# Seven block products in place of eight for gate and up of three FFNs and the convolution's input projection

## The chip, the cores and the metric

One NeuronCore of one Trainium2 chip runs the whole program in one launch. The metric is the time of one execution on the device in microseconds. The engines are TensorE (matrix products, "PE", its weight loads "PEld"), VectorE ("DVE"), ScalarE ("ACT"), GpSimd ("POOL") and SyncE ("SP", which issues most of the DMAs).

## The reference

Two layers of a causal decoder trunk, in float32. Each layer is FFN, mixer, FFN; the mixer of layer 0 is a diagonal state space model (S5) with a GLU, that of layer 1 a short gated convolution. 512 prompt tokens and 8 x 8 sample tokens go through the same weights.

```python
def _ffn_half(x, g, w_gu, w_down):
    h = _rmsnorm(x, g)
    gate, up = jnp.split(h @ w_gu, 2, axis=-1)      # w_gu: 1024 x 8192
    return (jax.nn.silu(gate) * up) @ w_down        # w_down: 4096 x 1024

def _conv_mixer(h, buf, w_in, conv_w, w_out):
    gb, gc, v = jnp.split(h @ w_in, 3, axis=-1)     # w_in: 1024 x 3072
    z = gc * v
    ...                                             # three taps along the tokens
    return (gb * conv) @ w_out, ...

# layer i: x += 0.5 ffn(x); x += mixer(rmsnorm(x)); x += 0.5 ffn(x); at the end an rmsnorm
```

## The kernel before, in words

**Layout.** All 576 tokens stay on the chip, features in partitions: `x` is 8 tiles of 128 features x 576 tokens. A product of a 128x128 weight tile with a tile of tokens is done in two halves of 288 columns (`NH`), and each half three times, because a float32 operand is split into a high part rounded to `F32R` and a low remainder: high weight x high tokens, low weight x high tokens, high weight x low tokens (`Step.mm`, line 128).

**Steps.** The work is a list of steps. A step has 8 weight tiles of 128x128, so 8 x 3 x 2 = 48 matmuls. A gate or up step makes one tile of 128 features from the 8 input tiles; a down step takes 4 tiles of h and adds to two tiles of x. One FFN is 8 groups of 8 gate and up steps and 4 down steps; the GLU has 16 steps, the convolution 24 for its input projection (c, v, b) and 8 for its output.

**Weights.** A `Unit` is 1 MB of weights, loaded by one DMA of SyncE into one of two `raw` buffers; it serves two steps. `split` (lines 116 and 117) makes a step's high half `wh` on ScalarE and its low half `wl` on VectorE, in one of four buffers each; it is called three steps ahead (`split_upto(n + 3)`).

**Order.** `tc.manual_schedule()` is on: each engine's instructions run in the order in which the Python code issues them. In the main loop step n is: split of step n+3, matmuls of step n, `finish(n)` with the epilogue. Results go to PSUM tiles of two banks (`[P, 2, 512]`, one bank a half), four of which rotate. The gate epilogue is a product with rstd (L205), Silu (L206) and again rstd (L207); up is a product (L214), the high half of h (L216) and its low half (L217); down adds to x (L223).

**Norms.** `next_norm` scales each final x tile by the norm's g into a high and low `xg` tile (L175, L176) and adds up squares (L168, L169) while the last down steps run; `start` issues the first matmuls of the next stage, then rstd (L182 to L193), which only the epilogues need.

**Buffers.** The pool `actp` has 20 tiles of 128x2x576; xg, h, the mixer's tables and its y take turns in it. The S5 constants lie in a pool that lives to the end, and the convolution borrows one of them (`trig`) for its shifted rows.

Of the kernel before, what the change touches and what calls it, by code (L numbers as in the profile page):

```python
# [33 lines left out]
def trunk_kernel(ctx: ExitStack, tc: tile.TileContext, a, o):  # L34
# [6 lines left out]
    actp = ctx.enter_context(tc.tile_pool(name="actp", bufs=20))  # L41
# [5 lines left out]
    dram = ctx.enter_context(tc.tile_pool(name="dram", bufs=1, space=bass.MemoryType.DRAM))  # L47
    ctx.enter_context(tc.manual_schedule())
# [7 lines left out]
    def ctile(shape, dt, name):  # L56
        return const.tile(shape, dt, name=name, tag=name)

# [15 lines left out]
    # ---------------------------------------------------------------- constants, parameters, x  # L74
# [15 lines left out]
    # ---------------------------------------------------------------- the stream of weights  # L90
# [12 lines left out]
    class Step:  # L103
# [15 lines left out]
        def mm(self, m, k, x, halves=(0, 1)):  # L119
            """The products of weight tile (k, m) with x, into the step's PSUM tile m."""  # L120
# [31 lines left out]
    # ---------------------------------------------------------------- norms  # L152
# [20 lines left out]
    def scaled_in(i, g):  # L173
        t = act(name="xg")
        S.activation(t[:, 0], x[:, i], AF.Copy, scale=g)  # L175
        late.append(lambda: stt(t[:, 1], x[:, i], g, raw32(t[:, 0]), op0=MUL, op1=SUB))  # L176
        return t
# [79 lines left out]
    def next_norm(n):  # L257
        def go(i):
            flush()
            if i == 0:  # L260
                state["xg_next"] = []
            state["xg_next"].append(scaled_in(i, gcol(n, i)))
            square_in(i)
            if i == NT - 1:
                state["xg"] = state["xg_next"]
        return go
# [4 lines left out]
    trig = ctile([P, 2, PAIRS * NK], F32, "trig")  # L271
    cosT, sinT = (trig[:, q].rearrange("p (t k) -> p t k", k=NK) for q in range(2))
    mag8 = ctile([P, PAIRS], F32, "mag8")
    s0 = ctile([P, G, NS], F32, "s0")
    ns = ctile([P, 2, NS, PAIRS], F32, "ns")
    hfin = ctile([P, G], F32, "hfin")
    scr = ctile([P, 2368], F32, "scr")
# [14 lines left out]
    dmask = ctile([P, 16], F32, "dmask")  # L292
    warm = ctile([P, 1], F32, "warm")
    strip = ctile([P, P + TC], F32, "strip")
    exi = ctile([P, PAIRS], I32, "exi")
# [19 lines left out]
    def exp_exact(out, z, t1, t2):  # L315
        """exp by range reduction and a polynomial, to float32's accuracy."""
# [138 lines left out]
    def bg_unit_powers():  # L455
        """cos and sin of 8 theta, their table over chunks, and |a|^8."""
# [56 lines left out]
    def bg_pw_rev():  # L513
        """Powers a^(7-j), j = 0..7, over (j, t) in rows."""
# [62 lines left out]
    def bg_q(i):  # L577
        """Rows of C a^n: real part, and minus the imaginary part."""
# [101 lines left out]
    # ---------------------------------------------------------------- S5: the mixer  # L680
# [8 lines left out]
    def ssm_bounce(i):  # L689
        """g x, from rows (g c) to rows (c j) by way of DRAM; the mean square of each token."""  # L690
# [4 lines left out]
        U = ss["U", i] = act([P, N], F32, "U")  # L695
# [6 lines left out]
    def chunk_rstd():  # L702
        """rstd of token (j, k) in rows (c j), column k."""
# [87 lines left out]
    def ssm_back(i):  # L791
        y = ss["y", i] = act(name="y")
        GP.dma_start(raw32(y[:, 1]), y_d[i].rearrange("g (c j) k -> (g c) (j k)", j=TC))
# [11 lines left out]
    def ssm(n):  # L805
        """The mixer, and the first four steps of the GLU, whose products follow y as it comes."""
# [46 lines left out]
        products((2, 3), (6, 7))  # L853
        state["xg"] = [ss["y", i] for i in range(NT)]
# [24 lines left out]
    # ---------------------------------------------------------------- GLU  # L879
    def glu():  # L880
# [8 lines left out]
        def gate(i):  # L889
            def go(ps):  # L890
# [4 lines left out]
                next_norm(2)(i)  # L895
# [13 lines left out]
    # ---------------------------------------------------------------- short convolution  # L909
    def conv():  # L910
        w_in, w_out = a["conv_w_in"][0], a["conv_w_out"][0]
        g, ps_t = {}, {}
        zp = trig[:, 0, 0:2 * W + N]
        cache = trig[:, 1, 0:128].rearrange("p (i e) -> p i e", e=16)
        zlast = trig[:, 1, 128:272].rearrange("p (i e) -> p i e", e=18)

        def load_cache():
            GP.memset(zp, 0.0)
            state["cache"] = act([16, D], F32, "cache_in")
            GP.dma_start(state["cache"], a["cache_conv"][0].rearrange("s w d -> (s w) d"))  # L920

        def turn_cache():
            t = state.pop("cache")
            ps = psum()
            for i in range(NT):
                T.transpose(ps[:, 0, i * 16:(i + 1) * 16], t[:, i * P:(i + 1) * P], ident[:16, :16])
            S.activation(cache, ps[:, 0, 0:P].rearrange("p (i e) -> p i e", e=16), AF.Copy)

        def scaled(key):
            def go(ps):  # L930
                t = tmpt(name="cv")
                V.tensor_mul(h2(t), ps[:, :, :NH], h2(state["rstd"]))
                g[key] = t
            return go

        def value(i):
            def go(ps):
                scaled(("v", i))(ps)
                z = zp[:, 2 * W:]
                V.tensor_mul(z, g.pop(("c", i)), g.pop(("v", i)))  # L940
                head = zp[:, 0:2 * W].rearrange("p (w k) -> p w k", w=2)
                S.activation(head[:, :, 0:NS], cache[:, i].rearrange("p (s w) -> p w s", w=2), AF.Copy)
                tail = zp[:, 8 * W:].rearrange("p (w k) -> p w k", w=2)
                S.activation(head[:, :, NS + 1:], tail[:, :, NS:W - 1], AF.Copy)
                zl = zlast[:, i].rearrange("p (w e) -> p w e", w=2)
                S.activation(zl[:, :, 0:NS], tail[:, :, 0:NS], AF.Copy)
                S.activation(zl[:, :, NS:], tail[:, :, W - 1:], AF.Copy)
                c = tmpt(name="conv")
                wv = [vecs[:, (GW + k) * 8 + i:(GW + k) * 8 + i + 1] for k in range(3)]
                V.tensor_scalar(c, zp[:, 0:N], wv[0], None, op0=MUL)  # L950
                stt(c, zp[:, W:W + N], wv[1], c, op0=MUL, op1=ADD)
# [362 lines left out]
```

## Time and profile before

| | |
|---|---|
| median of 3 runs | 2908.58 us (2908.33 to 2910.24) |
| span of the profiled execution | 2910.0 us |
| TensorE matmuls | 21694, busy 2872.7 us |
| VectorE, ScalarE busy | 1452.2 us, 799.7 us |
| from DRAM | 260.19 MB, 97 GB/s over the span |

The span runs from the first to the last instruction of one execution. Matmuls overlap in the array, so the mean time of one (296 ns) is longer than the distance between two. Idle time of an engine is put down to what ended it. Rows below are whole lines of the profile; "..." marks lines left out between them.

### The profile page before, as it was taken

How to read it: one execution, taken by the hardware profiler on the slowest of the kernel's cores; microseconds unless marked ns; L12 is line 12 of the kernel's file. 1: busy time of each engine (PE TensorE's matmuls, PEld its weight loads, DVE VectorE, ACT ScalarE, POOL GpSimd, SP SyncE). 2: the span in 40 equal slices, each digit the busy share in tenths (PEclk: the TensorE clock that was granted, in tenths of full speed). 3: DMA queues.
4: the chain of work that ended last, by engine and by line, in shares of the span. 5: the costliest groups of instructions: out<-in, count | busy, mean ns of one | idle time of the engine just before them, and what ended most of it. 6: DMA issues, size and time to landing. Idle time of an engine off the chain costs nothing.

```text
span 2910.0 us, 48733 instructions
## 1 busy us (share of the span) xinstructions
PE 2872.7 (99%) x21694; PEld 2858.2 (98%) x21694; DVE 1452.2 (50%) x1903; ACT 799.7 (27%) x1054; POOL 132.2 (5%) x208
## 2 busy tenths in 40 slices
PE   8999999998999999999999999999999999999998
PEld 8999999998999999999999999999999999999998
DVE  5667655549344444444544444444655544444444
ACT  4222243332332222222332222222323322222223
POOL 3000122102100000000000000000000000000000
PEclk9999999998999999999999999999999999999999
DMA  6355444447223222222222222222123222222221
GB/s 128 95 153 160 128 145 146 125 160 232 76 77 98 75 84 75 88 87 87 73 87 87 74 87 87 76 85 88 59 93 96 74 76 84 87 88 87 78 82 48
DMA packets 227105, 285.15 MB, mean 98 GB/s; under 512 B 17332, under 2 KB 179488, under 8 KB 226864
## 3 DMA queue, kind: packets, MB, share of 16 engines
q1 hardware_dynamic: 217504, 256.86, 28.6%
q0 software_dynamic: 9216, 24.98, 2.9%
q8 instruction: 171, 2.80, 0.4%
q10 hardware_dynamic: 176, 0.20, 0.1%
q14 instruction: 38, 0.31, 0.0%
HBM read 260.19 MB, written 21.80 MB: 97 GB/s over the span
## 4 chain that ended last, share of the span: by engine, by line
PE 96%; DVE 2%; issue 1%; DMA 0%; SPq 0%; ACT 0%; POOLq 0%; ACTq 0%; DVEq 0%
PE ps L128 94%; PE ps L1039 1%; DMA xin<-in_x_prompt_dram 0%; PE ps L785 0%; DVE scr L772 0%; PE ps L611 0%; DVE g L764 0%; DVE scr L773 0%; PE ps L784 0%; DVE xg L1239 0%; PE ps L1062 0%; DVE U L727 0%; PE ps L182 0%; DVE v L766 0%; DVE v L755 0%
## 5 line engine op out<-in xcount | busy, mean ns | idle before, releaser
L128 PE MATMUL ps<-xg,wh 128*128 128x288 f32 x8960 | 1569.2, 296 | 3.0 <-DVE xg L1239 3.0
L128 PEld LDWEIGHTS ps<-xg,wh 128*128 128x128 f32 x8960 | 1323.6, 189 | 6.2 <-DVE xg L1239 3.4
L128 PE MATMUL ps<-xg,wl 128*128 128x288 f32 x4480 | 959.8, 296 | 0.0
L128 PEld LDWEIGHTS ps<-xg,wl 128*128 128x128 f32 x4480 | 722.7, 189 | 0.0
L128 PE MATMUL ps<-h,wh 128*128 128x288 f32 x3968 | 695.2, 296 | 0.0
L117 DVE TENSOR_TENSOR wl<-raw,wh 128x1024 fp32r<-128x1024 f32 x432 | 529.9, 1227 | 232.1 <-ACT wh L116 232.1
L116 ACT ACTIVATE wh<-raw 128x1024 fp32r<-128x1024 f32 x432 | 453.4, 1050 | 613.3 <-PE ps L128 454.1
L128 PEld LDWEIGHTS ps<-h,wh 128*128 128x128 f32 x3968 | 586.2, 189 | 1.3 <-DVE x L223 1.3
L128 PE MATMUL ps<-h,wl 128*128 128x288 f32 x1984 | 424.8, 296 | 0.0
L223 DVE SCALAR_TENSOR_TENSOR x<-ps,x 128x576 f32<-128x576 f32 x248 | 187.1, 757 | 303.0 <-PE ps L128 301.7
L128 PEld LDWEIGHTS ps<-h,wl 128*128 128x128 f32 x1984 | 319.8, 189 | 0.0
L206 ACT ACTIVATE gate<-gate 128x576 f32<-128x576 f32 x128 | 87.7, 686 | 586.4 <-DVE gate L205 578.5
L205 DVE TENSOR_TENSOR gate<-ps,rstd 128x576 f32<-128x576 f32 x128 | 96.9, 757 | 300.9 <-PE ps L128 300.7
L216 ACT ACTIVATE h<-up 128x576 fp32r<-128x576 f32 x128 | 87.7, 685 | 571.8 <-DVE up L214 555.4
L214 DVE TENSOR_TENSOR up<-ps,gate 128x576 f32<-128x576 f32 x128 | 96.8, 757 | 264.3 <-PE ps L128 264.1
L217 DVE TENSOR_TENSOR h<-up,h 128x576 fp32r<-128x576 f32 x128 | 97.1, 758 | 96.9 <-ACT h L216 96.1
L207 DVE TENSOR_TENSOR gate<-gate,rstd 128x576 f32<-128x576 f32 x128 | 97.1, 759 | 96.4 <-ACT gate L206 96.4
L128 PE MATMUL ps<-y,wh 128*128 128x288 f32 x512 | 92.6, 302 | 0.0
L128 PEld LDWEIGHTS ps<-y,wh 128*128 128x128 f32 x512 | 77.8, 194 | 0.0
L128 PE MATMUL ps<-y,wl 128*128 128x288 f32 x256 | 55.8, 300 | 0.0
L920 POOL DMA_DIRECT2D cache_in<-in_cache_conv_dram x1 | 0.5, 525 | 1066.4 <-PE ps L128 1066.4
L128 PE MATMUL ps<-cg,wh 128*128 128x288 f32 x256 | 44.9, 296 | 0.0
(316 smaller groups left out, 1172.7 us busy)
## 6 DMA issues: line engine op xcount, KB each, us to landing
raw<-in_ffn_w_gate_up_dram SPq DMA_DIRECT2D x126, 1024.0 KB, 5.7
raw<-in_ffn_w_down_dram SPq DMA_DIRECT2D x64, 1024.0 KB, 5.1
raw<-in_conv_w_in_dram SPq DMA_DIRECT2D x12, 1024.0 KB, 5.1
raw<-in_ssm_w_glu_dram SPq DMA_DIRECT2D x8, 1024.0 KB, 5.4
pri<-pw_d SPq DMA_DIRECT2D x16, 256.0 KB, 8.8
bri<-bb_d SPq DMA_DIRECT2D x16, 256.0 KB, 8.7
ws_d<-ws POOLq DMA_DIRECT2D x8, 512.0 KB, 4.1
wy_d<-wy POOLq DMA_DIRECT2D x8, 512.0 KB, 2.9
```

What stands on the lines that cost most here:

```text
L116: S.activation(self.wh, src, AF.Copy)
L117: V.tensor_sub(self.wl, src, raw32(self.wh))
L128: T.matmul(self.ps[m][:, b, :NH], wt[:, k, c], x[:, part, b * NH:(b + 1) * NH], start=k == 0 and wt is self.wh and part == 0, stop=k == se ...
L205: V.tensor_mul(h2(t), ps[:, :, :NH], h2(state["rstd"]))
L206: S.activation(t, t, AF.Silu)
L207: V.tensor_mul(t, t, state["rstd"])
L214: V.tensor_mul(h2(t), ps[:, :, :NH], h2(gates.pop(d)))
L216: S.activation(h[:, 0], t, AF.Copy)
L217: V.tensor_sub(h[:, 1], t, raw32(h[:, 0]))
L223: V.scalar_tensor_tensor(h2(x[:, i]), ps[:, :, :NH], 0.5, h2(x[:, i]), op0=MUL, op1=ADD)
L920: GP.dma_start(state["cache"], a["cache_conv"][0].rearrange("s w d -> (s w) d"))
L1039: T.matmul(pst[i][:, 0, :NH], wt[:, k, m * P:(m + 1) * P], hs[k][:, part, cols], start=k == 0 and wt is st.wh and part == 0, stop=k == 3 a ...
```

## The change

The second, third and fourth FFN and the convolution no longer run as steps, apart from down and output products. Their gate, up and input weights are taken in units of 256 columns, and a unit's 1024x256 block is cut in four: 512x128 each (rows of the 8 input tiles alternate between the two halves). The tokens are cut in their two halves of 288. The eight block products of such a 2x2 by 2x2 product are replaced by seven (Strassen's scheme in Winograd's form), on sums of weight blocks and of token blocks; each is 4 x 3 = 12 matmuls of 288 columns, and the results are put together from running sums.

- `Seven` holds a unit. `make_r1`, `make_s12`, `make_r2`, `make_s4` are its weight chunks: sums on VectorE, high half on ScalarE, low half on VectorE. `pump` issues the next chunk as soon as one of four buffers (and one of one for s4) has been given up by the products issued so far.
- `product` issues the 12 matmuls. Q1, S2, S1 and S4 add up in one bank (`x`), S3 and Q4 in a second (`z`); Q2 has its own (`y`). `evacuate` follows each: ScalarE copies bank x after Q1, S2, S1 and S4, VectorE forms the other combinations, and Q4's is followed by the epilogue of the 256 columns (`gate`, `up`, or the convolution's).
- `stage` sets the order: Q1 of a unit, S4 of the one before, S3, Q4 of the one before, S2, Q2, S1; the four down steps of a group come behind S1 of every fourth unit.
- `feed` and `combine` take the place of `next_norm`: each pair of final x tiles is scaled, four sums are made, and seven blocks are split in high and low.
- Pools: S5's constants and `actp` (12 tiles now) are closed when the mixer ends and the new buffers lie in their place; xg, U and y of the earlier stages have a pool of their own, `xgp`.

The core of the diff, new code only:

```diff
+    def pump():
+        while chunks and live[chunks[0].tag] < cap[chunks[0].tag]:
+            c = chunks.pop(0)
+            live[c.tag] += 1
+            c.make()
...
+    class Seven:
+        TERMS = {"Q1": ("r1", 0, 0, "x"), "S3": ("r1", 1, 5, "z"), "S2": ("s12", 0, 4, "x"),
+                 "S1": ("s12", 1, 3, "x"), "Q2": ("r2", 0, 1, "y"), "Q4": ("r2", 1, 6, "z"),
+                 "S4": ("s4", 0, 2, "x")}
...
+        def make_r1(self):
...
+            V.tensor_add(st[:, :, 1], a21, a22)
+            V.tensor_add(a21, a21, a11)
+            V.tensor_add(st[:, :, 0], st[:, :, 1], a11)
+            self.w["r1"] = split_of(v[:, :, 0], 2, wp, ("wh", "wl"))
+
+        def make_s12(self):
+            self.s4f = late_tile("s4f", "s4f", [P, 4, 1, P], F32, "s4f")
+            V.tensor_add(self.s4f[:, :, 0], self.st[:, :, 0], self.v[:, :, 1, 0])
+            self.w["s12"] = split_of(self.st, 2, wp, ("wh", "wl"))
...
+            for k in ks:
+                t = state["tk"][k]
+                for wt, part in ((wh, 0), (wl, 0), (wh, 1)):
+                    T.matmul(ps, wt[:, k, sel], t[:, part, slot],
+                             start=term in ("Q1", "Q2", "S3") and k == 0 and wt is wh and part == 0,
...
+        def evacuate(self, term):
...
+                S.activation(self.q[:, 0], x_, AF.Copy)
+            elif term == "S2":
+                S.activation(self.q[:, 1], x_, AF.Copy)
+            elif term == "Q2":
+                V.tensor_add(self.c[:, 0, 0], self.q[:, 0], self.y)
+            elif term == "S1":
+                S.activation(self.q[:, 2], x_, AF.Copy)
+                stt(self.c[:, 1, 1], self.q[:, 2], -1.0, z_, op0=MUL, op1=SUB)
+            elif term == "S4":
+                S.activation(self.c[:, 0, 1], x_, AF.Copy)
+            elif term == "Q4":
+                stt(self.c[:, 1, 0], self.q[:, 1], -1.0, z_, op0=MUL, op1=SUB)
+                self.after(self.c.rearrange("p a b n -> p a (b n)"))
...
+    def combine(j, ba):
+
+        bt = big([P, 4, NH], "bt")
+        V.tensor_sub(bt[:, 0:3:2], ba[:, 0:3:2], ba[:, 3:4].to_broadcast([P, 2, NH]))
+        stt(bt[:, 1], bt[:, 0], -1.0, ba[:, 2], op0=MUL, op1=SUB)
+        stt(bt[:, 3], bt[:, 1], -1.0, ba[:, 1], op0=MUL, op1=SUB)
+        t = late_tile("tkr" if j < 3 else "tkl", "tk", [P, 2, 7, NH], F32R, "tk")
+        S.activation(t[:, 0, 0:3], ba[:, 0:3], AF.Copy)
+        V.tensor_sub(t[:, 1, 0:3], ba[:, 0:3], raw32(t[:, 0, 0:3]))
+        S.activation(t[:, 0, 3:7], bt, AF.Copy)
+        V.tensor_sub(t[:, 1, 3:7], bt, raw32(t[:, 0, 3:7]))
...
+            items.append(s.item("Q1"))
+            if prev:
+                items.append(prev.item("S4"))
+            items.append(s.item("S3"))
+            if prev:
+                items.append(prev.item("Q4"))
+            items += [s.item("S2"), s.item("Q2"), s.item("S1")]
+            items += inserts.get(n, [])
...
+        def gate(b):
+            def go(c):
+                V.tensor_mul(c, c, spread(state["rstd"]))
+                S.activation(c, c, AF.Silu)
...
+        def up(b):
+            def go(c):
+                g = gates.pop(b)
+                V.tensor_mul(g, g, spread(state["rstd"]))
+                V.tensor_mul(c, c, g)
+                h = late_tile("hp", "hp", [P, 2, 2, N], F32R, "h")
+                S.activation(h[:, 0], c, AF.Copy)
+                V.tensor_sub(h[:, 1], c, raw32(h[:, 0]))
...
+            it.run()
+            for c in it.chunks:
+                c.left -= 1
+                if c.left == 0:
+                    live[c.tag] -= 1
+            pump()
```

In the convolution `value` rescales 256 rows, then does the product, the shifts and the three taps for each of its two tiles; `gateb` multiplies into a float32 tile, which is split in high and low just ahead of the output products.

## Rows read from the trace of the kernel before

**Rows 1.** The page, part 1: busy us, share of the span, instructions.

```profile
PE 2872.7 (99%) x21694; PEld 2858.2 (98%) x21694; DVE 1452.2 (50%) x1903; ACT 799.7 (27%) x1054; POOL 132.2 (5%) x208
```

**Rows 2.** The page's chain that ended last, shares of the span by engine.

```profile
PE 96%; DVE 2%; issue 1%; DMA 0%; SPq 0%; ACT 0%; POOLq 0%; ACTq 0%; DVEq 0%
```

**Rows 3.** Pieces of that chain in order of time: start, length, instruction.

```profile
850.92 614.39 PE ps L128 x4608
```

**Rows 4.** Waits of ScalarE: who waited for whom; total us, times, longest.

```profile
ACT gate L206 <- DVE gate L205: 578.5, 126, 6.5
```

**Rows 5.** Groups by line and shape: busy us, mean ns of one, idle before.

```profile
L117 DVE TENSOR_TENSOR wl<-raw,wh 128x1024 fp32r<-128x1024 f32 x432 | 529.9, 1227 | 232.1 <-ACT wh L116 232.1
L116 ACT ACTIVATE wh<-raw 128x1024 fp32r<-128x1024 f32 x432 | 453.4, 1050 | 613.3 <-PE ps L128 454.1 <-issue 128.1 <-DMA raw<-in_ffn_w_gate_up_dram 25.1
...
L214 DVE TENSOR_TENSOR up<-ps,gate 128x576 f32<-128x576 f32 x128 | 96.8, 757 | 264.3 <-PE ps L128 264.1
...
L206 ACT ACTIVATE gate<-gate 128x576 f32<-128x576 f32 x128 | 87.7, 686 | 586.4 <-DVE gate L205 578.5 <-issue 7.9
...
L175 ACT ACTIVATE xg<-x,vecs 128x576 fp32r<-128x576 f32 x32 | 25.0, 781 | 70.8 <-DVE x L969 32.5 <-DVE x L223 23.9 <-DVE x L894 14.3
...
L1043 DVE SCALAR_TENSOR_TENSOR x<-ps,x 128x288 f32<-128x288 f32 x16 | 7.2, 458 | 9.6 <-PE ps L1039 9.6
...
L951 DVE SCALAR_TENSOR_TENSOR conv<-trig,vecs,conv 128x576 f32<-128x576 f32 x8 | 6.6, 820 | 0.3
...
L413 DVE TENSOR_TENSOR wst<-pri,bri 128x512 f32<-128x512 f32 x8 | 5.5, 693 | 0.3
...
L1051 ACT ACTIVATE sq<-x 128x288 f32<-128x288 f32 x12 | 5.1, 428 | 0.0
```

**Rows 6.** Timeline where one step ends and the next begins: start, length.

```profile
1013.95 0.43 PE L128 MATMUL ps<-xg,wh 128*128 128x288 f32 x2
...
1014.15 1.06 ACT L116 ACTIVATE wh<-raw 128x1024 fp32r<-128x1024 f32 x1 [5.28 <-PE ps L128]
```

**Rows 7.** Timeline of one gate's epilogue and the next weight split.

```profile
1021.34 0.69 ACT L206 ACTIVATE gate<-gate 128x576 f32<-128x576 f32 x1 [6.13 <-DVE gate L205]
...
1021.93 1.04 ACT L116 ACTIVATE wh<-raw 128x1024 fp32r<-128x1024 f32 x1
...
1023.01 1.23 DVE L117 TENSOR_TENSOR wl<-raw,wh 128x1024 fp32r<-128x1024 f32 x1 [0.19 <-ACT wh L116]
```

**Rows 8.** Timeline of two VectorE instructions with nothing to wait for.

```profile
1436.93 0.75 DVE L223 SCALAR_TENSOR_TENSOR x<-ps,x 128x576 f32<-128x576 f32 x1
...
1437.60 0.81 DVE L176 SCALAR_TENSOR_TENSOR xg<-x,vecs,xg 128x576 fp32r<-128x576 f32 x1
```

**Rows 9.** Timeline of the convolution's shifts.

```profile
2092.50 0.31 ACT L944 ACTIVATE trig<-trig 128x126 f32<-128x126 f32 x1 [5.12 <-DVE trig L940]
```

**Rows 10.** Timeline of VectorE over one rstd, its first and last instruction.

```profile
1466.33 0.76 DVE L184 TENSOR_SCALAR var<-ps 128x576 f32<-128x576 f32 x1 [2.60 <-PE ps L182]
...
1473.25 0.76 DVE L193 TENSOR_TENSOR rstd<-r,newt 128x576 f32<-128x576 f32 x1
```

**Rows 11.** Timeline of TensorE, start of the kernel: idle in brackets.

```profile
33.73 0.78 PE L128 MATMUL ps<-xg,wh 128*128 128x288 f32 x4 [1.97 <-DVE xg L1239]
```

**Rows 12.** Timeline of TensorE in the mixer, two gaps.

```profile
668.35 2.19 PE L736 MATMUL ps<-U,ws 128*64 128x72 f32 x32 [3.98 <-issue]
...
688.40 0.62 PE L785 MATMUL ps<-scr,wy 128*128 128x72 f32 x2 [2.63 <-issue]
```

**Rows 13.** Windows of TensorE: stretch, length, busy, granted clock, DMA share, GB/s.

```profile
33.00:35.00 2.00, 1.27 (x9) 1.00 0.83 229
668.00:670.00 2.00, 1.65 (x28) 0.50 1.00 310
690.00:692.00 2.00, 2.00 (x11) 0.50 1.02 410
736.00:738.00 2.00, 2.00 (x11) 0.50 0.43 106
```

More of the change, by code (lines that the diff above doesn't have):

```diff
@@ L47, in trunk_kernel @@
     dram = ctx.enter_context(tc.tile_pool(name="dram", bufs=1, space=bass.MemoryType.DRAM))
+    early, mid_left, late_r = ExitStack(), ExitStack(), ExitStack()
+    xgp = mid_left.enter_context(tc.tile_pool(name="xgp", bufs=8))
+    s5p = early.enter_context(tc.tile_pool(name="s5p", bufs=1, side="right"))
+    actp = early.enter_context(tc.tile_pool(name="actp", bufs=12, side="right"))
     ctx.enter_context(tc.manual_schedule())
@@ new lines, in open_left, with __init__ @@
+    def open_left():
+        mid_left.close()
+        for n, bufs in (("tkl", 1), ("hp", 2), ("s4", 1)):
+            B[n] = late_r.enter_context(tc.tile_pool(name=n, bufs=bufs, side="left", reuse_waits="tile"))
+        cap["s4"] = 1
+    class Chunk:
+        def __init__(self, tag, unit, make):
+            self.tag, self.unit, self.make, self.left, self.made = tag, unit, make, 0, False
+    class Item:
+        def __init__(self, chunks, run):
+            self.chunks, self.run = chunks, run
+            for c in chunks:
+                c.left += 1
@@ L997, in conv @@
-        starts.append(first)
-        steps[first - 12].post = load_cache
-        steps[first - 8].post = turn_cache
-        hs = lambda: [g["h", k] for k in range(NT)]
-        mid = len(steps)
-        for i in range(0, NT, 2):
-            uo = unit(w_out[:, i * P:(i + 2) * P], 8, 2 * P)
-            for s in range(2):
-                steps.append(Step(uo, s, hs, [out(i + s)]))
-        pairs.append(mid)
-        steps[mid + 1].post = rows_out
-    def tail(n):
-        last = steps[n:n + 4]
-        split_upto(n + 3)
+                    T.transpose(ps[:18, 0, k * P:(k + 1) * P], B["c_zlast"][:, hf * 4 + k], ident)
@@ new lines, in conv_items, with first @@
+        items = stage(sevens)
+        st = []
+        for i in range(0, NT, 2):
+            uo = Unit(w_out[:, i * P:(i + 2) * P], 8, 2 * P)
+            st += [Step(uo, s, lambda: [g["h", k] for k in range(NT)], [out(i + s)]) for s in range(2)]
+        cs = [step_chunk(t) for t in st]
+        def first():
+            for k in range(NT):
+                split_cg(k)
+                for t in st[:2]:
+                    t.mm(0, k, g["h", k])
+            for t in st[:2]:
+                t.evac[0](t.ps[0])
+            rows_out()
@@ new lines, in conv_items, with later, tail @@
+        return items + [Item(cs[:2], first)] + [step_item(t, c) for t, c in zip(st[2:], cs[2:])]
+    def later():
+        for it in late_items:
+            while not all(c.made for c in it.chunks):
+                n = len(chunks)
+                pump()
+                assert len(chunks) < n
+            pump()
+            it.run()
[3 more added lines that the diff above has]
+                    live[c.tag] -= 1
+            pump()
+    def tail(last):
@@ L1125, in trunk_kernel @@
     glu()
-    ffn(0, 1, next_norm(3))
-    ffn(1, 0, next_norm(4))
-    conv()
-    ffn(1, 1, lambda i: None)
     steps[last_ffn1 - 5].post = ssm_prefetch
+    late_items = late_ffn(0, 1, feed(3))
+    late_items += late_ffn(1, 0, feed(4), {8: load_cache, 10: turn_cache})
+    late_items += conv_items(feed(5)) + late_ffn(1, 1, None)
+    for it in late_items:
+        for c in it.chunks:
+            if c not in chunks:
+                chunks.append(c)
+                if c.unit not in units:
+                    units.append(c.unit)
     loaded, done = [0], [0]
@@ L1259, in trunk_kernel @@
     n = 0
-    while n < len(steps) - 4:
+    while n < len(steps):
         if n == 0:
@@ L1282, in trunk_kernel @@
         assert not bg or n < last_ffn1 - 5, len(bg)
-    tail(n)
+        if "big" in B and done[0] == len(steps):
+            live["w"] = len(steps) - n + sum(1 for c in made if c.tag == "w")
+            pump()
+    later()
+    late_r.close()
 _INS = ["x_prompt", "x_sample", "state_ssm_re", "state_ssm_im", "cache_conv", "norm_g", "final_norm_g",
```

370 lines of the change are left out of this document (267 added, 103 removed).

## The prediction

> **What bounds the kernel now.** I read the page first. Part 1 shows TensorE busy 99% of the span, VectorE 50%, ScalarE 27% [rows 1]; part 4 puts 96% of the chain that ended last on TensorE [rows 2]. Then the chain in order of time, for the pace: one unbroken piece covers 4608 products of 288 columns in 614.39 us, 133.3 ns each [rows 3]. So the kernel is as long as its count of matmuls, and the other two engines wait for TensorE. The waits say how: ScalarE stood 578.5 us in front of a Silu until VectorE had rescaled its input [rows 4], and that cost nothing. Then the groups by shape, for prices [rows 5], and the timeline for the hops between engines: ScalarE starts 0.20 after the place in TensorE's stream where a step is over [rows 6]; the next instruction of the same queue starts about 0.1 before the record of the one ahead ends, and one that waits for another engine about 0.03 after it [rows 7, 8].
>
> **What the change removes.** A unit of 256 weight columns takes 7 products of 12 matmuls in place of 96 matmuls. There are 32 units in each of three FFNs and 12 in the convolution: 108 x 12 = 1296 matmuls, at 133.3 ns [rows 3] 172.8 us. All of it lies on the path. One product is 12 x 133.3 ns = 1.60 us, a unit 11.2 us (12.8 before).
>
> **Prices of the added work**, from [rows 5]. VectorE: 128x1024 1.23, 128x576 0.757, 128x512 0.69, 128x288 0.46. Two of these give (1227-757)/448 = 1.05 ns an element, so 128x1152, which the trace lacks, is 0.757 + 576 x 1.05 = 1.36. It can't be under 1.23 (fewer elements) nor over two of 576, 1.51; I take 1.36. ScalarE: 1024 1.05, 576 0.69, 288 0.43, so 1152 is 1.15 and 512 0.63.
>
> **What it adds to the path.** Before, each result had two PSUM banks of its own, and four such tiles rotated: an epilogue could come late by a whole step. Now Q1, S2, S1 and S4 of a unit accumulate in one bank, and ScalarE must copy it out after each before TensorE may go on. Between S2 and S1 lies one product, Q2: 1.60 us. And in ScalarE's queue the copy after S2 stands behind whatever was issued before it: the high half of the next unit's r1, of s4, then, when Q4 of the unit before is over, that unit's Silu (gate) or its high half of h (up), then the high half of s12. Silu and h wait for VectorE, where the low halves of r1 and s4 stand first, and the first of these waits for ScalarE, which waits until S3 gives its weight buffer free (four buffers, four in use).
>
> I write the queues out over one frame, from the end of one unit's S3 (0) to the end of the next one's. After S3 come Q4 of the unit before, S2, Q2 (ends 4.80), S1, then Q1, S4 and S3 (four products, 6.40).
>
> Gate: r1 high 0.20 to 1.25 on ScalarE; r1 low 1.28 to 2.51 on VectorE, s4 low to 3.12, Q4's combination 3.04 to 3.50, rescaling 3.53 to 4.89; Silu 4.92 to 6.07; s12 high to 7.02; the copy of S2's bank to 7.35; S1 at 7.40. It could have gone at 4.80: **2.6 us of idle TensorE**. The frame is 7.40 + 6.40 = 13.8.
>
> Up: VectorE has one more 1152 (gate times rstd, then the product), 3.42 to 6.17; h high to 7.35, s12 high to 8.30, the copy to 8.63, S1 at 8.68: **3.9 us idle**, a frame of 15.1.
>
> Up with the down steps behind S1: r1 and s4 give way to the first down split (no s4 low), S1 at 8.1: **3.3 idle**; the down steps themselves run through.
>
> VectorE also fits its remaining work in such a frame, barely: in an up frame the h low half, two s12 pieces, two combinations, r2 low and three sums for the next r1 end at 15.0. It has no slack to give the time back.
>
> Each FFN has 29 such frames: 15 gate, 7 up, 7 up with downs: 15 x 2.6 + 7 x 3.9 + 7 x 3.3 = 89.4; three FFNs **+268**. The bound from below leaves r1 and s4 out of the way (Q4's combination at 1.80): 1.4 and 2.6 us, 57 an FFN, 172 in all. It isn't nothing, since the rest is one chain of in-order instructions.
>
> The Trainium skill, "TensorE: Matmul & The Clock Gate", in its opening table, says that TensorE's queue may reorder in part while ScalarE's and VectorE's are strict first in, first out. If they could pass a waiting instruction, the copy would run inside Q2 and the 268 would be 0. The 578.5 us in which ScalarE stood in front of the Silu [rows 4] fit the page's rule, but no row shows a ready instruction held behind a waiting one.
>
> **Edges of an FFN.** S2 of the third unit waits for its Q1 copy behind the second unit's epilogue (6.0 against 3.2): 2.8. Nothing stands between the last S1 and S4: 0.2 + 0.43 + hop = 0.7. The last down step needs h 6.0 us after the last Q4 and has 4.8 of other products: 1.2. Three times 4.7: **+14**.
>
> **Convolution.** Its `value` epilogue puts, before the copy, a rescaling (1.36) and two rounds of a product (0.757), ScalarE's shifts (0.31 [rows 9] and three shorter ones) and three taps (up to 0.82 [rows 5]) over one shared buffer: S1 at about 11.0, 6.2 idle. Three such frames, 18.6; the c and b units have no ScalarE work there and wait for nothing. At the end the output products wait 5.0 for combination, rescaling, two products and the first split. **+24**.
>
> **Starts after a norm.** Before, x tiles were scaled and split as the last down steps finished them, and TensorE did not wait: the piece in [rows 3] runs through to the next rstd. Now each pair of tiles costs VectorE two evictions (1.51), four sums and two splits of 864 and 1152 (4.1) and two sums of squares (1.5), 7.1 us, plus some 1.8 for ScalarE's scaled copies (0.78 [rows 5]); and r1, r2, r1 (3.3, 1.23, 3.3) of the next stage stand between: 43 us for four pairs, less the sums behind the last. A step gives 6.40. The last pair is ready some 20 us after the last down product; the first three pairs' products fill 6.0 of them: 14 lost. Then S1 waits for copies that stand behind Ln and Exp in the rstd chain (7.7 us on VectorE from first to last [rows 10]): 5 more. 19 for each of three starts and 7 after the GLU, where pairs come four steps apart: **+64**. From 8 to 30 each are possible.
>
> **TensorE's clock.** An idle of 1.97 us among products of 288 columns left the granted clock at full [rows 11, 13]; ones of 3.98 and 2.63 in the mixer were followed by half, 1.2 GHz [rows 12, 13], but among products of 72 columns. At 736 us products of 288 columns ran at half [rows 13], for about 4 us, a loss of 2. I take 1.5 lost in half of the 42 up frames and 2 at the four starts: **+40**; the ends are 0 and 2.0 at each wait, 182.
>
> **Sum.** -173 + 268 + 14 + 24 + 64 + 40 = +237. The span is 2910.0, so 3147; the median of the runs is 2908.6, 1.4 under the span, so **3145 us**. Lower bound: -173 + 172 + 14 + 12 + 32 + 0 = +57, 2965. Upper: -173 + 268 + 14 + 30 + 100 + 182 = +421, about 3330.
>
> **What costs nothing.** The weight loads: a unit's 1 MB is still fetched one unit ahead, and the span in which it must land grows. The smaller `actp` ring, the early stages and the mixer: the buffers taken out of it are the ones that moved to `xgp`; none of it touches the order there.
>
> **Rivals.**
> 1. The waits shorten: the splits of r1 and s4 run early enough that only the epilogue's own chain stands before the copy, and starts cost 8. For it: ScalarE is 27% busy now [rows 1]; against: the weight buffer is free only after S3. 2965 to 3040. Chance 0.17.
> 2. The clock stays low: each wait is followed by some 2 us lost, 3260 to 3330. For it: both gaps over 2.6 us [rows 12]; against: 1.97 was harmless among dense products. Chance 0.12.
> 3. Faster: the copy after S2 is not held by the epilogue, so it runs inside Q2 and TensorE waits only at edges and starts: -173 + 14 + 24 + 64 = -71, 2840. It decides as soon as frames take under 12.8. For it: VectorE's work for a gate and up pair (2 x (five of 512, three of 1024, three of 288) + four of 1152 = 22.5, less 0.08 of overlap each, 20.4) is under TensorE's 22.4; against: the order of the two queues. Chance 0.08.
> 4. Gain and waits cancel, within 0.2% (6 us; the runs differ by 2): 0.03.
> The forecast, 3050 to 3250, has 0.60. So slower by over 0.2% has 0.89, the same 0.03, faster 0.08. The range 2965 to 3300 leaves out rival 3, no change and the upper part of rival 2.
>
> **What would show it.** Right: TensorE busy well under 99%, with idle before products of S1, put down to ScalarE's copy out of the `x` bank, some 90 of them, 2.5 to 4 us each; gate and up pairs 29 us apart; gaps of over 10 us at three starts; granted clock below 1.00 in the three FFNs. Wrong: those waits under 1.6 us on average (then the saved 1.6 a unit is more than they cost), or an FFN under 615 us, what one takes now (the piece in [rows 3] and the four matmuls of its rstd).

## The result and the profile after

The changed kernel takes 3287.78 us (median of 4 runs, 3282.29 to 3292.95) against 2908.45 (2908.32 to 2910.24): a ratio of 1.1306, 95% interval 1.129 to 1.1322. It is slower, on the side and inside the range (2965 to 3300) that were forecast, 143 us above the predicted time and above the 3050 to 3250 that had the highest chance.

The page of the kernel after, part 1 (busy us, share of the span of 3291.1, instructions; the last line is the share of the chain that ended last, by engine):

```profile
PE 2872.5 (87%) x20398; PEld 2823.1 (86%) x20398; DVE 2041.4 (62%) x2719; ACT 1146.0 (35%) x1638; POOL 134.4 (4%) x213
...
PE 67%; DVE 18%; ACT 12%; issue 1%; DMA 0%; ACTq 0%; SPq 0%; POOLq 0%; DVEq 0%
```

Against [rows 1, 2] two things stand out. TensorE has 1296 matmuls fewer, as worked out, and yet it is busy for as long as before (2872.5 against 2872.7). And its idle has grown from 37.3 us (2910.0 - 2872.7) to 418.6. The whole change of the span, +381, equals the growth of the idle, +381; the 173 us that the matmuls took have been used up by slower matmuls. VectorE and ScalarE, which held 2% of the chain before, hold 30% of it.

Where TensorE waited in the kernel after (for what, total us, times, longest):

```profile
PE ps L1013 <- ACT q L1025: 280.6, 91, 6.1
PE ps L1013 <- ACT q L1023: 42.7, 12, 12.6
PE ps L1013 <- ACT c L1032: 28.5, 8, 8.3
PE ps L1013 <- DVE x L1132: 11.4, 4, 3.1
```

L1013 is the matmul of a block product, L1025 ScalarE's copy of bank x after S2, L1023 that after Q1, L1032 that after S4; L1132 adds a down step's result to x. The first line is the wait that the prediction wrote out.

The stretches of the last four stages after (FFN, FFN, convolution, FFN): length, TensorE busy, the other engines, granted clock, DMA:

```profile
828.00:1570.00 742.00, 622.96 (x4282) 611.51 (x4281) 458.89 (x557) 261.24 (x359) 1.03 (x2) 0.92 0.22 69
1570.00:2307.00 737.00, 621.63 (x4237) 610.61 (x4236) 448.69 (x545) 254.93 (x350) 0.00 (x0) 0.91 0.22 69
2307.00:2553.00 246.00, 204.57 (x1404) 200.07 (x1404) 183.66 (x241) 102.54 (x174) 4.03 (x8) 0.89 0.22 69
2553.00:3245.00 692.00, 582.60 (x4000) 573.92 (x4001) 411.99 (x498) 230.17 (x318) 0.00 (x0) 0.92 0.23 70
```

Read the third number with its count: 622.96 us over 4282 instructions is 145 ns each, where [rows 3] has 133.3. The granted clock is 0.89 to 0.92. From the rstd of one stage to that of the next (839.47, 1570.51 and 2307.84 in this trace) one FFN takes 731 to 737 us, where the piece in [rows 3] with its rstd took 615.

One up frame of the kernel after, VectorE, ScalarE and the product that waits (start, length; idle before and releaser in brackets):

```profile
1136.44 1.06 ACT L959 ACTIVATE wh<-raw 128x1024 fp32r<-128x1024 f32 x1 [1.23 <-PE ps L1013]
1137.41 0.62 ACT L959 ACTIVATE s4h<-s4f 128x512 fp32r<-128x512 f32 x1
1137.54 1.23 DVE L960 TENSOR_TENSOR wl<-raw,wh 128x1024 fp32r<-128x1024 f32 x1 [1.34 <-ACT wh L959]
1138.68 0.69 DVE L960 TENSOR_TENSOR s4l<-s4f,s4h 128x512 fp32r<-128x512 f32 x1
1139.28 0.45 DVE L1034 SCALAR_TENSOR_TENSOR c<-q,ps 128x288 f32<-128x288 f32 x1
1139.65 1.35 DVE L1120 TENSOR_TENSOR c<-c,rstd 128x1152 f32<-128x1152 f32 x1
1141.03 1.36 DVE L1121 TENSOR_TENSOR c<-c,c 128x1152 f32<-128x1152 f32 x1
1142.49 1.16 ACT L1123 ACTIVATE h<-c 128x1152 fp32r<-128x1152 f32 x1 [4.46 <-DVE c L1121]
1143.56 1.04 ACT L959 ACTIVATE wh<-st 128x1024 fp32r<-128x1024 f32 x1
...
1144.50 0.39 ACT L1025 ACTIVATE q<-ps 128x288 f32<-128x288 f32 x1
...
1144.94 0.50 PE L1013 MATMUL ps<-tk,wh 128*128 128x288 f32 x1 [3.83 <-ACT q L1025]
```

This is the predicted queue, entry by entry. From the end of S3 (1136.24, 0.20 ahead of the first line) to S1 it is 8.70 us, where 8.68 was written; TensorE is idle for 3.83, where 3.9 was. ScalarE stands 4.46 us in front of h (L1123), and the small copy that TensorE needs, whose bank S2 had long left, sits behind it. That is the row that was missing: a ready instruction held behind a waiting one. The strict first in, first out order of ScalarE that the Trainium skill states in the opening table of "TensorE: Matmul & The Clock Gate" holds here, and so does the price of 268 that hung on it.

The same stretch and the next frame in windows of 2 us (length, TensorE busy, granted clock, DMA share, GB/s):

```profile
1125.00:1127.00 2.00, 0.83 (x7) 1.00 0.00 0
1127.00:1129.00 2.00, 0.60 (x2) 0.76 0.00 0
1129.00:1131.00 2.00, 2.00 (x11) 0.50 0.03 8
1131.00:1133.00 2.00, 2.00 (x15) 0.89 0.00 0
...
1143.00:1145.00 2.00, 0.06 (x1) 1.00 0.00 0
1145.00:1147.00 2.00, 2.00 (x9) 0.53 0.00 0
1147.00:1149.00 2.00, 2.00 (x12) 0.62 0.00 0
1149.00:1151.00 2.00, 2.00 (x18) 1.00 0.00 0
...
1159.00:1161.00 2.00, 0.57 (x4) 1.00 0.00 0
1161.00:1163.00 2.00, 2.00 (x17) 1.00 0.00 0
```

Here is the term that was too small. Behind the gate frame's idle (2.56 us, until 1128.40) the clock is at half, 1.2 GHz, and two windows hold 26 products instead of some 35; behind the up frame's (until 1144.94) they hold 21. Behind the third (2.56 us as well, until 1160.43) nothing is lost. From 1128.40 to 1160.43 one gate and up pair without down steps takes 32.0 us, idle 6.4 of them; the prediction had 28.9, idle 6.5. The 3.2 us between are the clock. The Trainium skill tells this of another kernel, in bf16 with 512 columns (same page, "A second HAM failure mode: psum-queue depth-cycling"): short idles of TensorE between groups of matmuls, as it cycles through PSUM, make the clock fall again and again. This trace agrees, with 0.50 after idles of 2.56 and 3.83. It also shows that not every idle does it. Counted over the whole trace, half clock followed 26 of the 42 idles of 2.56 us before S1, 17 of the 22 of 3.23, all 20 of 3.83, and none of the four of under 2 us.

### The profile page after: what moved, and what is told of

It is laid out like the page before. It is cut to its first block, busy times and chain, and to the rows that moved or that the text cites. A ratio compares the mean times of both kernels' runs of the same rounds, so it can differ in the third digit from the quotient of the medians.

```text
span 3291.1 us, 47376 instructions
## 1 busy us (share of the span) xinstructions
PE 2872.5 (87%) x20398; PEld 2823.1 (86%) x20398; DVE 2041.4 (62%) x2719; ACT 1146.0 (35%) x1638; POOL 134.4 (4%) x213
## 4 chain that ended last, share of the span: by engine, by line
PE 67%; DVE 18%; ACT 12%; issue 1%; DMA 0%; ACTq 0%; SPq 0%; POOLq 0%; DVEq 0%
PE ps L138 39%; PE ps L1013 25%; ACT wh L959 5%; DVE wl L960 3%; DVE c L1121 2%; DVE c L1112 2%; DVE c L1120 2%; ACT h L1123 2%; ACT c L1113 2%; ACT wh L126 2%; DVE s4l L960 1%; DVE c L1034 1%; DVE wl L127 1%; ACT q L1025 1%; PE ps L1358 1%
## 5 line engine op out<-in xcount | busy, mean ns | idle before, releaser
L1013 PE MATMUL ps<-tk,wh 128*128 128x288 f32 x5184 | 1194.1, 319 | 370.8 <-ACT q L1025 280.6
L1013 PEld LDWEIGHTS ps<-tk,wh 128*128 128x128 f32 x5184 | 937.8, 208 | 400.9 <-ACT q L1025 302.0
L1013 PE MATMUL ps<-tk,wl 128*128 128x288 f32 x2592 | 820.0, 316 | 0.0
L138 PE MATMUL ps<-h,wh 128*128 128x288 f32 x3968 | 707.4, 299 | 1.2 <-DVE h L1124 1.2
L138 PEld LDWEIGHTS ps<-h,wh 128*128 128x128 f32 x3968 | 599.3, 193 | 3.4 <-DVE h L1124 1.7
L1013 PEld LDWEIGHTS ps<-tk,wl 128*128 128x128 f32 x2592 | 540.7, 209 | 0.5
L138 PE MATMUL ps<-h,wl 128*128 128x288 f32 x1984 | 430.6, 299 | 0.0
L138 PE MATMUL ps<-xg,wh 128*128 128x288 f32 x2048 | 362.0, 297 | 1.9 <-DVE xg L1564 1.9
L138 PEld LDWEIGHTS ps<-h,wl 128*128 128x128 f32 x1984 | 326.2, 192 | 0.0
L138 PEld LDWEIGHTS ps<-xg,wh 128*128 128x128 f32 x2048 | 303.4, 190 | 4.5 <-DVE xg L1564 2.2
L1132 DVE SCALAR_TENSOR_TENSOR x<-ps,x 128x576 f32<-128x576 f32 x184 | 138.6, 756 | 228.5 <-PE ps L138 228.5
L138 PE MATMUL ps<-xg,wl 128*128 128x288 f32 x1024 | 219.8, 296 | 0.0
L1013 PE MATMUL ps<-tk,s4h 128*128 128x288 f32 x864 | 190.9, 297 | 6.3 <-DVE c L1030 6.3
L138 PEld LDWEIGHTS ps<-xg,wl 128*128 128x128 f32 x1024 | 165.6, 190 | 0.0
L1013 PEld LDWEIGHTS ps<-tk,s4h 128*128 128x128 f32 x864 | 146.4, 191 | 8.0 <-DVE c L1030 8.0
L1029 ACT ACTIVATE q<-ps 128x288 f32<-128x288 f32 x108 | 44.3, 411 | 269.9 <-PE ps L1013 269.9
```

What stands on the lines that cost most here:

```text
L138: T.matmul(self.ps[m][:, b, :NH], wt[:, k, c], x[:, part, b * NH:(b + 1) * NH], start=k == 0 and wt is self.wh and part == 0, stop=k == se ...
L1013: T.matmul(ps, wt[:, k, sel], t[:, part, slot], start=term in ("Q1", "Q2", "S3") and k == 0 and wt is wh and part == 0, stop=k == 3 and pa ...
L1132: stt(h2(x[:, i]), ps[:, :, :NH], 0.5, h2(x[:, i]), op0=MUL, op1=ADD)
```

## The experiments

The theory after the result: the *order* of ScalarE's and VectorE's work delays the bank copies, and the idle that this makes costs clock on top. The expectations call it A; each says what it means there. One rival: TensorE's longer matmuls have another cause than its idle. The other: the two engines have too much to do for seven products, so that a wait taken away comes back at the next bank.

**x1_fill: work in TensorE's idle time.** Products into a spare tile, whose result nobody uses, stand between Q2 and S1.

```diff
+    def fill_in(s, count):
+        ps, w = psum(), s.w["s12"][0]
+        for _ in range(count):
+            T.matmul(ps[:, 0, :], w[:, 0, 0], ..., start=True, stop=True)
...
-            items += [s.item("S2"), s.item("Q2"), s.item("S1")]
+            items += [s.item("S2"), s.item("Q2")]
+            if fill and fill(n):
+                items.append(Item([], lambda s=s, c=fill(n): fill_in(s, c)))
+            items.append(s.item("S1"))
```

> The changed kernel with extra matmuls of 512 columns, whose results are not read, put into TensorE's queue between Q2 and S1 of every unit from the third on: 10 in frames with a gate epilogue, 15 with an up epilogue, 13 where down steps follow, 22 in the convolution's value frames. They fill part of the idle time in which TensorE waits for ScalarE's copy after S2. Theory A (the waits come from the order in ScalarE's queue, and the matmuls that took 319 instead of 296 ns ran at a granted clock that the waits had lowered): the frames stay as long as their chain, but the products in them run at full clock, so 130 to 165 us go and the time is 3120 to 3160; mean of an S1 matmul back near 296 ns; granted clock of the FFNs 0.98 or more. Rival B (the block products are slower for another reason, such as the way their operands lie or traffic from VectorE): the time stays at 3290 or rises, with mean matmul still near 319 ns.

Measured: 3182.59 us, ratio 1.0943 (1.0912 to 1.0975): 105 less than the kernel after, with 1104 matmuls more. The kernel's own products (busy us, mean ns), first after, then x1_fill:

```profile
L1013 PE MATMUL ps<-tk,wh 128*128 128x288 f32 x5184 | 1194.1, 319 | 370.8 <-ACT q L1025 280.6 <-ACT q L1023 42.7 <-ACT c L1032 28.5
```

```profile
L1013 PE MATMUL ps<-tk,wh 128*128 128x288 f32 x5184 | 1107.0, 302 | 123.6 <-ACT q L1023 40.4 <-ACT q L1025 33.0 <-ACT c L1032 28.5
```

Such groups overlap in time, so their busy times can't be added. All matmuls of L1013 taken together (span, length, TensorE busy, weight loads busy, granted clock, DMA), again first after, then x1_fill:

```profile
0.00:3291.10 3291.10, 1367.50 (x9072) 1329.95 (x9072) 0.93 0.29 87
```

```profile
0.00:3179.40 3179.40, 1266.82 (x9072) 1232.00 (x9072) 0.97 0.30 90
```

The same products on the same data are 101 us shorter once idle time is filled with useless ones, and the matmuls of the steps (L138) 18 us, 1371.6 in place of 1389.8. From 828 to 1500 us, in the first of the three FFNs, the granted clock is 0.98 in place of 0.93. So the idle slows the products behind it, and the rival, by which the time stays, falls. The 105 are less than the 130 to 165 of the theory: the fills stand only before S1, so the waits at L1023 and L1032, most of them at the starts of the stages, remain (40.4 and 28.5 us), and with them the clock lost there (0.86 granted from 1490 to 1550 us, over one such start); 33.0 us of waits remain at L1025.

**x2_s2_first: S2 ahead of Q4 of the unit before.**

```diff
             items.append(s.item("S3"))
+            items.append(s.item("S2"))
             if prev:
                 items.append(prev.item("Q4"))
-            items += [s.item("S2"), s.item("Q2"), s.item("S1")]
+            items += [s.item("Q2"), s.item("S1")]
```

> The changed kernel with one move: S2 of a unit is issued ahead of Q4 of the unit before, so that ScalarE's copy after S2 stands in its queue in front of that unit's epilogue, and two products lie between S2 and S1. Nothing else differs. Theory A (the wait is the copy held behind the epilogue in ScalarE's queue): the waits at S1 fall from 281 us to under 40, what is left is VectorE's own work, some 12.0 us a gate frame and 13.3 an up frame instead of 13.8 and 15.1 plus the lost clock; time 2980 to 3060. Rival C (VectorE's work, not the order, sets the length of a frame): frames stay over 14 us, time 3200 or more.

Measured: 3121.54, ratio 1.0733 (1.0702 to 1.0765). Neither. The wait for S2's copy went from 281 to 3.4 us, so the order did cause it; but S4 now waits. The first wait of x2_s2_first, then a frame of it:

```profile
PE ps L1013 <- DVE c L1030: 163.3, 72, 7.5
```

```profile
1120.27 1.17 ACT L1124 ACTIVATE h<-c 128x1152 fp32r<-128x1152 f32 x1 [4.37 <-DVE c L1122]
1121.34 1.04 ACT L959 ACTIVATE wh<-st 128x1024 fp32r<-128x1024 f32 x1
...
1122.29 0.39 ACT L1029 ACTIVATE q<-ps 128x288 f32<-128x288 f32 x1
...
1124.85 0.45 DVE L1030 SCALAR_TENSOR_TENSOR c<-q,ps 128x288 f32<-128x288 f32 x1
...
1125.36 0.61 PE L1013 MATMUL ps<-tk,s4h 128*128 128x288 f32 x1 [3.55 <-DVE c L1030]
```

S1's copy (L1029) is late by the same h, and its combination (L1030), behind the epilogue on VectorE, later still. S4 waits for that combination although S4 writes bank x and L1030 reads bank z: the two banks are one tile of the program.

**x3_pool_sums: the four block sums of a unit on GpSimd.**

```diff
-            V.tensor_add(st[:, :, 1], a21, a22)
+            GP.tensor_add(st[:, :, 1], a21, a22)
...
-            V.tensor_add(self.s4f[:, :, 0], self.st[:, :, 0], self.v[:, :, 1, 0])
+            GP.tensor_add(self.s4f[:, :, 0], self.st[:, :, 0], self.v[:, :, 1, 0])
```

> The changed kernel with the four sums of weight blocks of each unit (128x512 each) on GpSimd instead of VectorE; the order of all queues is otherwise the same. Theory A (the order in ScalarE's queue): the sums are not in the chain from S3 to the copy after S2, so the time moves by under 40 us either way, unless GpSimd is so slow that r1 comes late. Rival C (VectorE's work sets the length of a frame): 4 x 0.69 = 2.8 us a unit go from VectorE, up to 240 us over 87 frames, time near 3050. A third outcome, that VectorE slows down while GpSimd reads the same memory, would show as longer VectorE instructions (mean of the 1024 split over 1.3 us) and a time over 3330.

Measured: 3385.71, ratio 1.1642 (1.1565 to 1.1719), slower by 98 than the kernel after. Groups of x3_pool_sums by shape:

```profile
L982 POOL TENSOR_TENSOR st<-st,raw 128x512 f32<-128x512 f32 x108 | 193.1, 1788 | 0.0
...
L960 DVE TENSOR_TENSOR s4l<-s4f,s4h 128x512 fp32r<-128x512 f32 x108 | 108.2, 1002 | 15.8 <-ACT s4h L959 15.8
```

An up frame of x3_pool_sums, an epilogue product on VectorE and the S1 that waits:

```profile
1152.19 2.30 DVE L1121 TENSOR_TENSOR c<-c,c 128x1152 f32<-128x1152 f32 x1
...
1157.05 0.61 PE L1013 MATMUL ps<-tk,wh 128*128 128x288 f32 x1 [6.70 <-ACT q L1025]
```

A sum takes 1.52 to 1.79 us on average there, by spans that are rough on GpSimd (0.69 on VectorE), and VectorE's instructions beside them take longer: its split of s4 went from 685 to 1002 ns on average, the product L1121 in this frame from 1.36 to 2.30 us. Both stand in the chain to the copy, so S1 waits 6.70 us where 3.83 stood, and the wait at L1025 grew from 281 to 327 us in all; the granted clock over the span fell from 0.93 to 0.91. This is the third outcome of the expectation. Taking work off VectorE this way tells nothing on whether it is too full, since it lengthens the chain.

**x4_late_epilogue: x2, and a unit's epilogue and the next splits are issued behind S1's evacuation** (not where down steps need h at once).

```diff
-                self.after(self.c.rearrange("p a b n -> p a (b n)"))
+                after = lambda: self.after(self.c.rearrange("p a b n -> p a (b n)"))
+                if self.defer:
+                    hold.append(after)
...
             items.append(s.item("S3"))
+            items.append(s.item("S2"))
             if prev:
+                prev.defer = n not in inserts
                 items.append(prev.item("Q4"))
-            items += [s.item("S2"), s.item("Q2"), s.item("S1")]
+            items += [s.item("Q2"), s.item("S1"), Item([], late_epilogue)]
```

> As the kernel with S2 first, but the epilogue of the unit before (rescaling, Silu or h) and the next weight chunks are issued only behind S1 and its evacuation, except in frames with down steps, which need h at once. So both S1 (held by ScalarE's copy after S2) and S4 (held there by VectorE's combination after S1) have their evacuation in front of the epilogue in the queues. Theory A (the idle time is evacuations held behind an epilogue in an in-order queue): the waits at S1 and S4 fall together from 167 us to under 60, time 2990 to 3080. Rival C (VectorE's own work is the length of a frame, about 14 us): TensorE waits elsewhere instead (for weight chunks), time 3100 or more.

Measured: 3168.38, ratio 1.0893 (1.0857 to 1.093). A miss: worse than x2, and in the range of the rival. Waits of x4_late_epilogue (L1026 is now the copy after Q1, L1035 that after S4):

```profile
PE ps L1016 <- ACT q L1026: 242.4, 77, 12.6
PE ps L1016 <- ACT c L1035: 41.5, 8, 8.3
```

The waits of S1 for S2's copy and of S4 for VectorE are down to 2.7 and 4.0 us, but the whole epilogue now stands ahead of Q1's copy, one product on. So far the rival of full engines looked right: the wait had moved twice, though to a bank copy and not to the weight chunks that the rival named.

**x5_split_epilogue: x4 with the epilogue cut in two**: VectorE's products first, then the next splits, then Silu or the split of h.

```diff
-            hold.pop(0)()
+            rest = hold.pop(0)()
+            pump()
+            if rest:
+                rest()
...
-                S.activation(c, c, AF.Silu)
                 gates[b] = c
+                return lambda: S.activation(c, c, AF.Silu)
```

> As the kernel with the late epilogue, but the epilogue is cut in two: its products on VectorE, then the next weight chunks, then the part that begins on ScalarE (Silu; high and low half of h). VectorE no longer stands about 1.2 us in front of ScalarE's high half of h, nor in front of the high half of s12 behind a Silu. If what is left of the frames after the late epilogue is VectorE's queue with its waits: 1.2 to 1.6 us in each of 66 frames, 60 to 110 us under the kernel with the late epilogue. If VectorE is not the bound any more there: within 20 us of it.

Measured: 3006.25, ratio 1.0336 (1.0306 to 1.0366), 162 less than x4 where 60 to 110 were expected: the same instructions, and the wait at L1026 fell from 242.4 to 124.2. Here that rival begins to fail, since nothing was taken off any engine.

**x6_start_joined: x5, and the second unit of a stage joins the usual order.**

```diff
-                                         ("Q4", g), ("S4", u), ("Q4", u))]
-        prev = None
+                                         ("Q4", g))]
+        prev = u
```

> As the kernel with the split epilogue, but the second unit of a stage is not finished ahead of the third: its S4 and Q4 are taken into the ordinary order. In the changed kernel each start had a wait of 8.3 us of Q4 for ScalarE's copy of the other bank, behind a Silu, and one of 7.2 (12.6 in the convolution) of the third unit's first evacuation behind the second's epilogue. Theory A: most of these go, 4 x 10 to 15 us, 35 to 60 us under the kernel with the split epilogue. Rival (VectorE is behind after the norm anyway, and the wait only moves on): under 15 us.

Measured: 2970.55, ratio 1.0213 (1.0184 to 1.0243), 36 less than x5, at the low end of what was expected. The longest waits at the starts, 12.6 for Q1's copy and 8.3 for S4's, fell to 6.2 and 6.4, and those for S4's copy from 35.8 us in 8 to 9.3 in 4. What was left, in a gate frame of x6_start_joined:

```profile
1036.39 1.05 ACT L962 ACTIVATE wh<-st 128x1024 fp32r<-128x1024 f32 x1
...
1037.34 1.05 ACT L962 ACTIVATE wh<-raw 128x1024 fp32r<-128x1024 f32 x1
...
1038.34 1.17 ACT L1132 ACTIVATE c<-c 128x1152 f32<-128x1152 f32 x1
...
1039.41 0.39 ACT L1026 ACTIVATE q<-ps 128x288 f32<-128x288 f32 x1
...
1039.86 0.40 PE L1016 MATMUL ps<-tk,wh 128*128 128x288 f32 x1 [0.65 <-ACT q L1026]
```

ScalarE works without a gap from 1036.39 on; the copy is last of four.

**x7_rest_late: x6, and that last part goes behind Q1's copy.**

```diff
-            items.append(s.item("Q1"))
+            items += [s.item("Q1"), Item([], late_rest)]
```

> One edit on x6: ScalarE's and VectorE's last part of an epilogue (Silu of a gate, or the split of h) is issued behind the next unit's Q1 and its copy, in place of ahead of them. In x6 TensorE still waits 113 us x80 for the copy of Q1 (0.65 us in a gate frame, 2.04 in an up frame), which stands behind that Silu (1.07 us) or copy of h (1.41) and two weight copies. Theory A (the waits are ScalarE's order, and what is left of the loss is these waits and the clock they cost): the copy's wait falls to 15 to 40 us, the granted clock rises above 0.98, and the time to 2850 to 2900, below the kernel before for the first time. Theory C (ScalarE and VectorE are too full for seven products, so each wait that is taken away comes back at the next bank): another group of waits of over 60 us takes its place, 2935 to 2980.

Measured: 2911.26, ratio 1.0011 (1.0001 to 1.0021): the kernel before, to a tenth of a per cent. That is 59 less than x6, and 11 above A's end; the clock rose only to 0.974 (from 0.972), and L1026 kept 60.8 us in 38 waits, of them one of about 6.1 in each frame behind a `value` unit.

**x8_conv_split and x9_first_late: the last two places.** In x8 the convolution's `value` epilogue comes a tile at a time, behind the next copy after an S4 and the next after an S2; in x9 the first unit's epilogue of a stage goes by the late order too.

```diff
+                V.tensor_mul(cc, cc, c)
+                def half(s):
...
-                    V.tensor_mul(z, cc[:, s], c[:, s])
+                    S.activation(z, cc[:, s], AF.Copy)
...
+                def first():
+                    half(0)
+                    return lambda: half(1)
+                return lambda: first
```

```diff
+        g.defer = True
+        items.append(Item([], late_epilogue))
         prev = u
```

> Two edits on x7, both in the convolution alone: gate times value becomes one product of both tiles in place (VectorE), and the copy into the padded tile, the shifts and the three taps of each tile come a tile at a time, behind S4's copy and behind S2's copy of the next unit, in place of both tiles in one piece ahead of Q1's copy. In x7 that copy keeps TensorE 6.1 us in each of the four frames behind a value unit (24 us), and the stage's stretch has a granted clock of 0.94. Theory A (a strict order on ScalarE and VectorE is all that these waits are): the four fall below 1 us each and the time to 2870 to 2895, under x7 and under the kernel before by 0.4 to 1.3%. Theory C (the work has to be done somewhere in the frame, and the next bank waits instead): 2900 to 2915.

> x8, and the first unit's epilogue in each stage goes by the late order too (its Silu, with the 1.28 us table load ahead of it, behind the next unit's Q1 copy). In x7 that place costs 3.82 us at the start of each of the three FFNs (a wait for Q1's copy behind the table load, the Silu and a weight copy). Theory A: 8 to 15 us under x8. Theory C: within 5 us of x8, since those waits come back at S4's or S2's copy behind the same Silu.

Measured: x8 2896.84, ratio 0.9956 (0.9941 to 0.9971), the four waits of 6.1 gone, 2 above A's end; x9 2881.09, ratio 0.99 (0.9883 to 0.9916), 16 under x8, a little over A's 8 to 15. The page and the first waits of x9_first_late:

```profile
PE 2744.7 (95%) x20398; PEld 2700.4 (94%) x20398; DVE 2020.2 (70%) x2715; ACT 1128.9 (39%) x1646; POOL 135.3 (5%) x213
```

```profile
PE ps L1016 <- ACT q L1026: 33.3, 35, 1.2
PE ps L1016 <- ACT q L1028: 14.3, 27, 1.2
```

Seven products, the same splits and epilogues, in another order: 407 us less than the kernel after and 28 less than the kernel before. VectorE and ScalarE do as much as in the changed kernel (2020 and 1129 us busy against 2041 and 1146), so the rival of full engines (C in the expectations) is wrong: the work fits, and the order was the cost. Of the 172.8 us of removed matmuls x9 keeps 29.8 in its profiled span (2880.2 against 2910.0): 44.8 go to longer busy time (2744.7, where 2872.7 - 172.8 = 2699.9 would be at the pace of the kernel before; the granted clock over the span is 0.980, before 0.992), and 98.2 to idle (135.5 against 37.3), in many waits of about 1 us and the starts of the stages.

## Why the prediction came out as it did

**What it removes.** Right: 21694 - 20398 = 1296 matmuls.

**What it adds to the path.** Right in mechanism, place and size. For the wait at S1 it had 268 us in 87 frames of the FFNs and 18.6 in three of the convolution, 286.6 in 90; the trace has 280.6 in 91. That the order of the queues made it is shown by x2 (281 to 3.4 when S2 is moved) and by x9. The condition of rival 3, that the copy after S2 is not held by the epilogue, is met in x2, but there S4 waited in its place; the time that comes nearest to rival 3's 2840 is x9's 2881, after the order was rewritten in steps. Rival 1's early splits never came.

**Edges, convolution, starts.** Near in sum, by parts that differ. The rest of the idle is 381 - 281 = 100 us; the prediction had 14 + 5.4 + 64 = 83. At one FFN's start the waits are 11.3 us ahead of rstd and these two behind it (kernel after):

```profile
1592.46 1.16 ACT L1113 ACTIVATE c<-c 128x1152 f32<-128x1152 f32 x1
1594.48 0.39 ACT L1032 ACTIVATE c<-ps 128x288 f32<-128x288 f32 x1
...
1594.92 0.61 PE L1013 MATMUL ps<-tk,wh 128*128 128x288 f32 x1 [8.31 <-ACT c L1032]
...
1607.38 0.61 PE L1013 MATMUL ps<-tk,wh 128*128 128x288 f32 x1 [7.16 <-ACT q L1023]
```

In all 26.8, where 19 and, for the third unit's S2, 2.8 stood. Ahead of rstd it was less than forecast (11.3 against 14), and the two waits behind rstd were sized at 5 + 2.8. The 8.31 was not foreseen: the second unit's Q4 writes bank z and waits for the copy of bank x of its tile after its S4, which stands behind the first unit's Silu (a table load of 1.28 us in front). The sign of single gaps over 10 us at three starts did not come: the only one is 12.6, for Q1's copy in the convolution.

**TensorE's clock.** Here it failed, in size. The step took 1.5 us in half of the up frames and 2 at four starts, 40 in all, from an idle of 1.97 that cost nothing and a lack of longer ones among dense products [rows 11 to 13]. Measured: TensorE's busy time did not fall by the 172.8 of the removed matmuls, so some 172 were lost to half clock, 119 of them given back by x1_fill (101 + 18). The step left the gate frames out, but one of the two shown above lost clock too: 3.2 us for that gate and up pair, where the step had 0.75 on average. An estimate from the clock's records of this trace (half of TensorE's busy time at half clock) puts some 118 us behind 63 of the FFNs' S1 waits, where the step had 31.5 behind 21 up frames, and some 50 at the starts and in the convolution, where it had 8. The 132 that this term lacks, and the 11 of the idle (370 forecast, 381 measured), make the 143 by which the time was missed. The upper end of the term, 182, and the price of rival 2 (3260 to 3330, chance 0.12) are what happened, though a loss did not follow each wait; the doubt was in the text, the likeliest value was read from too few rows. That the time still fell inside the range is owed to that upper end.

**"It has no slack to give the time back"**, said of VectorE, is wrong as a reason: x9 gives most of it back with VectorE at 70%. It was true of this order only.

**What costs nothing.** Right: TensorE waits for no weight's DMA; its only waits for a DMA in the trace after are 5.0 and 1.4 us for an input and a norm's row at the start of the kernel.

## What to carry to other kernels

Before taking matmuls out of a kernel that TensorE bounds, count the small copies that it must wait for, and write out the in-order queue in which each of them stands; a copy of 0.4 us behind a Silu that waits for another engine cost 2.6 to 3.8 us a unit here, more than the 1.6 saved. Price a repeated idle like those here (2.56 us and more) twice, once as idle and once as clock, unless a trace shows that idle among like products to be harmless. And when a wait moves as an order is changed, look at what stands ahead of the new one before taking it that an engine is full: here it moved twice and then went.

## What was not expected of the hardware

- The clock falls behind idles of 2.56 us among dense products of 288 columns, to 0.50, for some 2 to 4 us, but not behind each of them (26 of 42; none lost after 1160.43). That such idles repeat every 14 to 17 us makes most of the 172 us.
- A product waits for another engine's read of the *other* bank of the same two-bank tile (S4 in x2 for VectorE's read of bank z, 3.55 us; Q4 above, 8.31). This is the program's own guard, as the rows show it; the Trainium skill ("PSUM — Partial Sum Buffer", "PSUM bank collisions raise a hardware error") asks for a guard by bank and partition quadrant, or more simply by bank, and no run here had the two banks as tiles of their own, so what a finer guard is worth stays open.
- GpSimd's sums slow VectorE beside them: a split with two inputs went from 685 to 1002 ns on average in x3, a product of 1152 columns in the frame shown from 1.36 to 2.30 us.
